# Two edits to a hybrid diffusion step: modulation row SH2 of layer 0 summed by VectorE, and other orders at the changes of phase

## The chip, the cores and the metric

The kernel runs on one core of one Trainium2 chip. Its time is device time in microseconds (us) of one execution of the whole program; the number used is the median of several executions. Five engines work side by side, each on its own queue of instructions: TensorE (PE) does matmuls, VectorE (DVE) and ScalarE (ACT) elementwise work, GpSimd (POOL) and SyncE (SP) issue transfers here. PSUM holds the results of matmuls; the 16 DMA engines move data between main memory and the on-chip SBUF.

## The reference

One step of a two-layer backbone on 128 context tokens and 256 latent tokens (384 columns together), width D = 2048, all in float32:

```python
for l in range(2):
    sh1, sc1, g1, sh2, sc2, g2 = split(silu(cvec) @ w_ada[l] + b_ada[l])   # six rows of 2048 per stream
    h = rmsnorm(x, norm_mix[l]) * (1 + sc1) + sh1
    mix = mixer_ab(h) if l == 0 else pool_mixer(h)   # attention + bidirectional HGRN2, or pooling
    x = x + g1 * mix
    h = rmsnorm(x, norm_mlp[l]) * (1 + sc2) + sh2
    x = x + g2 * (square(relu(h @ w_mlp_in[l])) @ w_mlp_out[l])
return rmsnorm(x, final_norm), new_k, new_v, new_s_fwd, new_s_bwd
```

The HGRN2 mixer keeps a 128x128 state for each of 8 heads in both directions, with forget gates; attention has 8 query heads on 2 key heads. Every row of the six (SH1, SC1, G1, SH2, SC2, G2) is a vector times a matrix of 2048 x 2048, for two vectors: the context's and the latent tokens'.

## The kernel before, in words

**Units and halves.** Weights stream through the chip as a list of items. One unit is 1 MB of weights, loaded by SP into one of three buffers `raw` (L139). A unit has two halves. For an ordinary unit each half is split into two rounded parts, high by ACT (`sp<-raw`, L166) and low by DVE (`sp<-raw`, L173), and PE runs 24 matmuls of 128x384 on them (`acc`, L273, L274, L276), or 36 of 128x256 where tokens are the rows (L403 to L405). Splits run four halves ahead of the matmuls. A `raw` buffer is loaded again only when both halves of its unit have been read, so the unit three places on waits for that.

**Units of the six rows.** An ada unit is 1 MB of `w_ada`. Where PE sums it (`ada_pe`), a unit is one group of four matmuls `psa<-raw,cpad` (L449), four units make a block of 512 columns, and the block is evacuated by ACT (`adarow`) and sent by POOL into the tile `folded`. Where DVE sums it (`ada_dve`), each half is two instructions over 128x1024 (`adaacc`; the first pair of a block TENSOR_SCALAR, L550, the others SCALAR_TENSOR_TENSOR, L552), and after eight units one group of four matmuls adds up the partitions (L566). The work of an ada unit is issued when the splits pass its place in the list, straight behind the low split of the half before it. In layer 0, G1, SH2 and SC2 are summed by PE, as 48 units spread over the mixer's items; G2 and layer 1's rows by DVE during the MLPs.

**Stages.** Start: the tokens are loaded, turned by PE (`px`, L725), their norm computed, SH1 and SC1 summed on PE (L501). Then the mixer of layer 0, 56 items behind the first: pairs of HGRN heads, attention's Q, K and V, four gates, sixteen output units; then MLP 0, pool mixer, MLP 1, final norm.

**An HGRN head** goes through seven levels. At each, PE makes `pl`, DVE updates `arr`, `tot` and `att`, ACT makes `kh`, and PE needs these for the next `pl`. After the last level come the two `arr` instructions (L993, L994), PE's output `po`, ACT's copies `sout`, DVE's `COPY O` (L1011). After two heads a norm follows: ACT's square root `oss` (L1021), DVE's RECIPROCAL and `O<-O,oss` (L1025), then PE's `pbh` (L1029), which stands in PE's queue ahead of the next matmuls.

**A change of phase** (before MLP 0, the pool mixer and MLP 1) computes the norm of `x`: ACT squares it (`sq`), DVE adds the squares (`sqacc`), PE sums over partitions (`pst`, L805), ACT takes the root (`rstd`, L809), DVE its reciprocal, PE spreads it (`pbc`, L827), DVE multiplies (`xnc`), ACT and DVE make `hh` and `hl`. PE runs filler matmuls (`busy`, L822) meanwhile.

Everything is in an order written by hand: a queue per engine, taken from the front. Background tasks (queues e, h, q, f) are advanced at given numbers of ticks.

Of the kernel before, what the change touches and what calls it, by code (L numbers as in the profile page):

```python
# [18 lines left out]
P = 128  # L19
# [20 lines left out]
LEAD = 6  # L40
WARM = (4, 3, 7)
WARM_START = 8
HY1 = 4.0
# [3 lines left out]
SPILL = 10  # L47
RAW_RING = 3
DMA_AHEAD = 6

# [64 lines left out]
class Model:  # L115
    def __init__(self, ctx, tc, a):
        self.ctx, self.tc, self.nc, self.a = ctx, tc, tc.nc, a
        self.items = []
        self.pend = []
        self.sqs = []  # L120
        self.queues = {"e": [], "h": [], "q": [], "f": []}
        self.now = 0.0
# [90 lines left out]
    def run(self):  # L213
# [7 lines left out]
        for j in range(2 * len(self.items)):  # L221
# [28 lines left out]
            if it["kind"] == "a" or (it.get("one") and half):  # L250
# [4 lines left out]
                continue  # L255
            if half == 0 and it["pre"]:
                self.flush()
                it["pre"]()
# [65 lines left out]
    def start_units(self, w, specs, pre=None):  # L324

        tiles = {}

        def make(q, n):
            def proc(half, sp):
                if q == 0:  # L330
                    tiles[n] = self.acc_pair()
                self.quarter_mm(tiles[n], sp, q, q == 0, q == 3)
                if q == 3:
                    self.pend.append(lambda: specs[n][1](tiles[n]))
            return proc

        return [self.quarter(w, specs[n][0], q, make(q, n), pre) for q in range(4) for n in range(len(specs))]

# [97 lines left out]
    def ada_pe(self, layer, which, block, each=None, then=None):  # L436
# [5 lines left out]
        def make(u):  # L442
            def proc(half, raw):
# [11 lines left out]
                if u == 3 and half == 1:  # L455
                    if layer == 0 and which in (SH1, SC1):
                        self.drain("f")
                    rows = self.small.tile([P, 512], F32, name="adarow", tag="adarow")
                    nc.scalar.activation(rows, st["ps"], AF.Copy)
                    if layer == 0 and which in (SH1, SC1):  # L460
                        self.task("f", finish(rows), PSRD)
                        if block == 0:
                            self.drain("f")
                    else:
                        if block == 0:
                            self.folded = self.small.tile([P, P], F32, name="folded", tag="folded", bufs=2)
                        for v in range(2):
                            at = block * 32 + v * 16
                            nc.gpsimd.dma_start(self.folded[at:at + 16], rows[v::32].rearrange("j (n c) -> j n c", n=4))
                        if block == 3:  # L470
                            self.task("f", self.ada_fold(layer, which, 0, P, self.folded), 6.5)
            return proc
# [63 lines left out]
    def ada_dve(self, layer, which, block):  # L536
# [5 lines left out]
        def make(u):  # L542
            def proc(half, raw):
                kc = u * 2 + half
                if kc == 0:
                    st["acc"] = self.mlpp.tile([P, 2, 1024], F32, name="adaacc", tag="adaacc")
                for v in range(2):
                    s = self.cpad[:, kc, v:v + 1]
                    if kc == 0:
                        nc.vector.tensor_scalar(st["acc"][:, v], raw[:, 0], s, None, op0=ALU.mult)  # L550
                    else:
                        nc.vector.scalar_tensor_tensor(st["acc"][:, v], raw[:, 0], s, st["acc"][:, v],  # L552
                                                       op0=ALU.mult, op1=ALU.add)
                if kc == KC - 1:
                    self.task("f", finish(), 4.0)
            return proc

        def finish():
            if block == 0:
                self.folded = self.small.tile([P, P], F32, name="folded", tag="folded", bufs=2)  # L560
            folded = self.folded
            psr = self.ps_a.tile([P, 512], F32, name="psa", tag="a")
            for v in range(2):
# [120 lines left out]
    def start_x(self):  # L684
# [7 lines left out]
        nc.vector.reciprocal(ss, ss)  # L692
        self.ss = ss

    def spread_x(self):
# [4 lines left out]
    def first_work(self, part, i):  # L700

        if part == 0:
            self.turn_x(2 * i)
            self.turn_x(2 * i + 1)
        if (part, i) in self.later:
# [13 lines left out]
    def turn_x(self, kc):  # L719
# [4 lines left out]
        for t in range(3):  # L724
            nc.tensor.transpose(ps[:, t], x[:, t], self.ident)  # L725
        if kc % 2:
            nc.vector.tensor_copy(x, ps)
# [55 lines left out]
    def square_into(self, kcs, late=False):  # L783
# [4 lines left out]
        for kc in kcs:  # L788
            sq = self.sqp.tile([P, T], F32, name="sq", tag="sq", bufs=3)
            nc.scalar.activation(sq, self.x[:, kc], AF.Square)  # L790
            self.sqs.append(sq)
        if kcs[0] < 2 and len(self.sqs) == 2:
            self.sqacc = self.sqp.tile([P, T], F32, name="sqacc", tag="sqacc", bufs=1)
            add(self.sqacc, self.sqs.pop(0), self.sqs.pop(0), op=ALU.add)
        while kcs[0] > 1 and len(self.sqs) > (late or kcs[-1] == KC - 1):
            add(self.sqacc, self.sqacc, self.sqs.pop(0), op=ALU.add)

    def norm(self):

        nc = self.nc  # L800
        self.keep_busy(WARM[0])
        ps = self.ps_s.tile([P, 3, 2], F32, name="pst", tag="s")
        for b in range(3):
            for n, t in enumerate([self.sqacc] + self.sqs):
                nc.tensor.matmul(ps[:, b], t[:, b * P:(b + 1) * P], self.ones[:, 0:2], start=(n == 0),  # L805
                                 stop=(n == 1))
        self.sqs = []
        r = self.tmp.tile([P, 3], F32, name="rstd", tag="rstd", bufs=1)
        nc.scalar.activation(r, ps[:, :, 0], AF.Sqrt, bias=self.eps, scale=1.0 / D)  # L809
        nc.vector.reciprocal(r, r)  # L810
# [407 lines left out]
    def open_mix(self):  # L1218
# [11 lines left out]
        self.nc.gpsimd.dma_start(self.ck, self.a["cache_k"][0, 0])  # L1230
        self.nc.gpsimd.dma_start(self.V[:, 3], self.a["cache_v"][0, 0].rearrange("t h d -> t (h d)"))
        self.hg_ctx = ExitStack()
        self.hg = self.hg_ctx.enter_context(self.tc.tile_pool(name="hgp", bufs=1))
# [6 lines left out]
    def open_x(self):  # L1240
# [6 lines left out]
        self.sqp = xp  # L1247
        self.task("q", self.read_x(), 1.0)

    def read_x(self):  # L1250

        for k in range(0, KC, 4):
            for b in range(3):
                self.nc.gpsimd.dma_start(self.x[:, k:k + 4, b * P:(b + 1) * P],
                                         self.x_spill[:, b, k * P:(k + 4) * P].rearrange("p (k t) -> p k t", t=P))
            yield 3.8

# [18 lines left out]
    def out_jobs(self):  # L1276
        w = self.a["w_out_ab"][0]
        for half, m in ((1, "mixA"), (0, "mixB")):
            for p in range(8):
                def evac(ps, os=(0, 1), p=p, half=half):  # L1280
                    for o in os:
                        self.add_x(2 * p + o, ps[o], self.part(0, G1))
# [90 lines left out]
    def pool_jobs(self):  # L1373
# [4 lines left out]
        for g in range(4):  # L1378
# [27 lines left out]
            src = w[g].rearrange("(k p) c -> p k c", p=P)  # L1406
            self.w_unit(src, (4, 512), proc, self.pool_pre if g == 0 else None)

# [71 lines left out]
    def build(self):  # L1480
# [103 lines left out]
```

## Time and profile before

| | us |
|---|---|
| median of three runs | 3092.82 (3092.79 to 3094.85) |
| the profiled execution, its time | 3093.35 |
| its span in the profile | 3091.6 |
| PE busy | 3041.5 (98%) |
| DVE busy | 1874.4 (61%) |
| ACT busy | 1153.5 (37%) |
| mean granted TensorE clock | 0.997 of full speed |

The profiled execution took 1.75 us more than its span, for what lies around it. The page gives busy time of each engine, the span in 40 slices, the chain of work that ended last, and groups of like instructions; the trace behind it gives every instruction with start, duration and what it waited for.

### The profile page before, as it was taken

Reading aid. Unit: us, or ns where it says so; the run is one execution under the profiler, and the core shown is the slowest. Engines: PE = TensorE matmul, PEld = TensorE weight load, DVE = VectorE, ACT = ScalarE, POOL = GpSimd, SP = SyncE. Lnnn points to the kernel's source line nnn. Section 1 sums busy time; section 2 is a strip of 40 time slices with the busy share of each in tenths; the row PEclk is TensorE's granted clock in tenths of the full one; section 3 lists DMA queues with packets and bytes.
Section 4 is the critical chain, followed back from the end, with each engine's and each line's share of the span. In section 5 each row is a group of like instructions: output and inputs, shape, how many; then the busy total and the mean of one; then the engine's idle time right before and its main releaser. Section 6 shows DMA issues by size and latency. Waiting matters only on the chain.

```text
span 3091.6 us, 43344 instructions
## 1 busy us (share of the span) xinstructions
PE 3041.5 (98%) x18074; PEld 2911.9 (94%) x18074; DVE 1874.4 (61%) x2448; ACT 1153.5 (37%) x1745; POOL 80.3 (3%) x137
## 2 busy tenths in 40 slices
PE   7999999999999999999999999999999999999997
PEld 4898999988999999999999999799999999999997
DVE  3555555555578988898998345754445444443444
ACT  3443333343453333323233333653333323333233
POOL 1100000010000000000000000000000000000000
PEclk9999999999999999999999999999999999999999
DMA  9964555564567777777777454254454444443452
GB/s 339 350 196 163 179 175 176 176 199 160 170 219 247 247 245 245 245 245 245 247 248 248 136 161 129 98 164 140 148 161 152 150 137 158 155 144 123 129 166 80
DMA packets 423764, 579.44 MB, mean 187 GB/s; under 512 B 11432, under 2 KB 348312, under 8 KB 422928
## 3 DMA queue, kind: packets, MB, share of 16 engines
q1 hardware_dynamic: 409728, 543.91, 54.3%
q0 software_dynamic: 8784, 28.29, 2.6%
q10 hardware_dynamic: 5056, 4.47, 0.5%
q8 instruction: 142, 2.33, 0.3%
q14 instruction: 54, 0.44, 0.0%
HBM read 562.42 MB, written 13.89 MB: 186 GB/s over the span
## 4 chain that ended last, share of the span: by engine, by line
PE 95%; DVE 2%; ACT 2%; DMA 1%; issue 0%; SPq 0%; DVEq 0%; ACTq 0%
PE acc L273 28%; PE acc L276 28%; PE acc L274 28%; PE psa L449 2%; PE pl L971 1%; DMA raw<-in_w_ada 1%; PE acc L403 1%; PE acc L405 1%; PE acc L404 1%; PE psa L566 0%; ACT hfull L765 0%; ACT sp L166 0%; PE acc L295 0%; DVE sp L173 0%; PE pov L1209 0%
## 5 line engine op out<-in xcount | busy, mean ns | idle before, releaser
L166 ACT ACTIVATE sp<-raw 128x1024 fp32r<-128x1024 f32 x656 | 694.2, 1059 | 1444.4 <-PE acc L276 1191.0
L173 DVE TENSOR_TENSOR sp<-raw,sp 128x1024 fp32r<-128x1024 f32 x656 | 795.7, 1222 | 590.6 <-ACT sp L166 590.3
L273 PE MATMUL acc<-hh,sp 128*128 128x384 f32 x2720 | 923.3, 339 | 3.2 <-ACT hh L767 1.5
L274 PE MATMUL acc<-hh,sp 128*128 128x384 f32 x2720 | 909.9, 335 | 0.0
L276 PE MATMUL acc<-hl,sp 128*128 128x384 f32 x2720 | 691.3, 335 | 0.0
L273 PE MATMUL acc<-hid,sp 128*128 128x384 f32 x2032 | 686.3, 338 | 0.0
L274 PE MATMUL acc<-hid,sp 128*128 128x384 f32 x2032 | 683.2, 336 | 0.0
L273 PEld LDWEIGHTS acc<-hh,sp 128*128 128x128 f32 x2720 | 510.8, 188 | 51.2 <-issue 39.0
L276 PE MATMUL acc<-hid,sp 128*128 128x384 f32 x2032 | 518.9, 337 | 0.0
L552 DVE SCALAR_TENSOR_TENSOR adaacc<-raw,cpad,adaacc 128x1024 f32<-128x1024 f32 x420 | 511.6, 1279 | 0.0
L274 PEld LDWEIGHTS acc<-hh,sp 128*128 128x128 f32 x2720 | 511.0, 188 | 0.1
L276 PEld LDWEIGHTS acc<-hl,sp 128*128 128x128 f32 x2720 | 491.4, 188 | 0.0
L273 PEld LDWEIGHTS acc<-hid,sp 128*128 128x128 f32 x2032 | 381.4, 188 | 5.9 <-issue 5.9
L274 PEld LDWEIGHTS acc<-hid,sp 128*128 128x128 f32 x2032 | 381.5, 188 | 0.0
L276 PEld LDWEIGHTS acc<-hid,sp 128*128 128x128 f32 x2032 | 367.3, 188 | 0.0
L777 DVE TENSOR_TENSOR hid<-rsq,hid 128x384 fp32r<-128x384 f32 x128 | 65.8, 555 | 195.0 <-ACT hid L776 195.0
L1359 DVE TENSOR_TENSOR x<-acc,x 128x384 f32<-128x384 f32 x192 | 97.8, 551 | 86.9 <-PE acc L276 86.9
L953 ACT ACTIVATE kh<-arr 128x384 f32<-128x384 f32 x56 | 31.2, 558 | 180.0 <-DVE arr L976 80.8
L449 PE MATMUL psa<-raw,cpad 128*32 128x512 f32 x576 | 78.0, 603 | 2.6 <-DMA raw<-in_w_ada 2.6
L976 DVE TENSOR_TENSOR arr<-arr,tot 128x384 f32<-128x384 f32 x96 | 49.2, 554 | 40.9 <-PE pl L971 39.6
L403 PE MATMUL acc<-sp,hh 128*128 128x256 f32 x240 | 72.7, 303 | 0.0
L1337 ACT ACTIVATE rsq<-relu 128x384 f32<-128x384 f32 x128 | 67.4, 526 | 4.1
(283 smaller groups left out, 2139.1 us busy)
## 6 DMA issues: line engine op xcount, KB each, us to landing
raw<-in_w_ada SPq DMA_DIRECT2D x192, 1024.0 KB, 5.1
raw<-in_w_mlp_out SPq DMA_DIRECT2D x128, 1024.0 KB, 5.5
raw<-in_w_mlp_in SPq DMA_DIRECT2D x120, 1024.0 KB, 5.5
raw<-in_w_in_ab SPq DMA_DIRECT2D x42, 1024.0 KB, 5.1
raw<-in_w_out_ab SPq DMA_DIRECT2D x16, 1024.0 KB, 5.6
raw<-in_w_mlp_in SPq DMA_DIRECT2D x16, 512.0 KB, 3.9
raw<-in_w_in_ab POOLq DMA_DIRECT2D x15, 512.0 KB, 7.3
x_kept<-x POOLq DMA_DIRECT2D x8, 768.0 KB, 3.6
```

The lines of the kernel that those rows point to most:

```text
L166: self.nc.scalar.activation(sp[:, 0], raw, AF.Copy)
L173: self.nc.vector.tensor_tensor(sp[:, 1], raw, sp[:, 0].bitcast(F32), op=ALU.subtract)
L273: mm(ps[:, :T], sp[:, 0, kc, c], hi, start=first, stop=False)
L274: mm(ps[:, :T], sp[:, 1, kc, c], hi, start=False, stop=False)
L276: mm(ps[:, :T], sp[:, 0, kc, c], lo, start=False, stop=last)
L403: nc.tensor.matmul(ps, hi, sp[:, 0, kc], start=(gk == 0), stop=False)
L449: nc.tensor.matmul(st["ps"][32 * j:32 * j + 32], self.cpad[:, kc], raw[:, k], start=(u == 0), stop=(u == 3))
L552: nc.vector.scalar_tensor_tensor(st["acc"][:, v], raw[:, 0], s, st["acc"][:, v], op0=ALU.mult, op1=ALU.add)
L777: nc.vector.tensor_tensor(lo, full, hi.bitcast(F32), op=ALU.subtract)
L976: nc.vector.tensor_tensor(x, x, m, op=ALU.mult)
L1337: nc.scalar.activation(q[o], r[o], AF.Square)
L1359: nc.vector.tensor_tensor(self.x[:, kc], ps[o][:, :T], self.x[:, kc], op=ALU.add)
```

## The change

One part hands SH2 of layer 0 to DVE. Its sixteen units go behind items picked by hand (`QUIET`, counted from the first HGRN item of pair 1; a number twice means two units there). G1 and SC2 stay on PE, as 32 units spread over the items. `adaacc` gets its own memory, and the folding matmuls use another PSUM pool.

The other part reorders the changes of phase and the start. In the norm, `pst` runs over the squares in the outer loop and the tokens in the inner one, so that only three matmuls need the last square; before MLP 1 the last four squares aren't added by DVE, and PE sums them (15 matmuls). The norm is issued ahead of the splits of the items that follow ("early"). At the start, four of the sixteen turns of the tokens go ahead of the first SH1 group, with their copies on DVE. The re-read of `x` in the mixer (3 MB) is cut into 24 transfers, three every 6.5 ticks, where 12 went out together. Fillers are fewer (`WARM`, `WARM_START`), and the memory for software DMA descriptors is set to 8192.

```diff
-WARM = (4, 3, 7)
-WARM_START = 8
+WARM = (4, 3, 4)
+WARM_START = 6
+QUIET = (0, 9, 10, 20, 20, 28, 36, 37, 38, 38, 39, 49, 50, 51, 52, 53)
...
-            if half == 0 and it["pre"]:
+            if half == 0 and it["pre"] and "early" not in it:
...
+        units[0]["early"] = pre
...
                 if kc == 0:
-                    st["acc"] = self.mlpp.tile([P, 2, 1024], F32, name="adaacc", tag="adaacc")
+                    self.drain("f")
+                    st["acc"] = self.accp.tile([P, 2, 1024], F32, name="adaacc", tag="adaacc")
...
-            psr = self.ps_a.tile([P, 512], F32, name="psa", tag="a")
+            psr = self.ps_bg.tile([P, 512], F32, name="psa", tag="bg")
...
         self.ss = ss
+        for kc in range(4):
+            self.turn_x(kc)
...
-        if part == 0:
-            self.turn_x(2 * i)
-            self.turn_x(2 * i + 1)
+        if part == 0 and i < 6:
+            self.turn_x(2 * i + 4)
+            self.turn_x(2 * i + 5)
...
-        if kc % 2:
+        if kc % 2 or kc < 4:
             nc.vector.tensor_copy(x, ps)
...
+        if late and kcs[0] >= KC - 4:
+            return
...
-        for b in range(3):
-            for n, t in enumerate([self.sqacc] + self.sqs):
-                nc.tensor.matmul(ps[:, b], t[:, b * P:(b + 1) * P], self.ones[:, 0:2], start=(n == 0),
-                                 stop=(n == 1))
+        for n, t in enumerate([self.sqacc] + self.sqs):
+            for b in range(3):
+                z = 6 + HEADS - 1 - b
+                nc.tensor.matmul(ps, t[:, b * P:(b + 1) * P], self.sel[:, z:z + 4], start=(n == b == 0),
+                                 stop=(n == len(self.sqs) and b == 2))
...
-        for k in range(0, KC, 4):
+        for k in range(0, KC, 2):
             for b in range(3):
...
-            yield 3.8
+            self.x_read += 1
+            yield 6.5
...
-        self.items = mix[:n0] + spread(mix[n0:], pe(G1, SH2, SC2), 0, len(mix) - n0 - 3)
+        body, quiet = mix[n0:], dve((0, SH2))
+        steps = len(body) - 3
+        own = pe(G1, SC2)
+        out, done = [], 0
+        for n, it in enumerate(body):
+            want = min(n * len(own) // steps, len(own))
+            out += own[done:want]
+            done = want
+            out.append(it)
+            for _ in range(QUIET.count(n)):
+                out.append(quiet.pop(0))
+        self.items = mix[:n0] + out + own[done:] + quiet
...
-    nc = _bacc.Bacc("TRN2", target_bir_lowering=False, num_devices=1)
+    nc = _bacc.Bacc("TRN2", target_bir_lowering=False, num_devices=1, dynamic_dma_scratch_size=8192)
```

The first place where the order moves is DVE at the end of the fourth HGRN head and the norm of that pair (`O<-po` is the head's output, `oss` the norm's factor, `pbh` comes from PE). Before:

```order
297 L993 TENSOR_SCALAR arr<-arr,tot 128x128
298 L994 TENSOR_SCALAR arr<-arr,tot 128x128
299 L173 TENSOR_TENSOR sp<-raw,sp 128x1024
300 L1011 COPY O<-po 128x384
301 L1022 RECIPROCAL oss<-oss 128x6
302 L1025 TENSOR_TENSOR O<-O,oss 128x384
```

After:

```order
298 L1004 TENSOR_SCALAR arr<-arr,tot 128x128
299 L1005 TENSOR_SCALAR arr<-arr,tot 128x128
300 L558 SCALAR_TENSOR_TENSOR adaacc<-raw,cpad,adaacc 128x1024 x8
301 L175 TENSOR_TENSOR sp<-raw,sp 128x1024
302 L1022 COPY O<-po 128x384
303 L1033 RECIPROCAL oss<-oss 128x6
304 L1036 TENSOR_TENSOR O<-O,oss 128x384
```

Two units of SH2, eight instructions, now stand between the head's last `arr` and its `COPY O`.

The second place is DVE at the end of the last head, with the same names. Before:

```order
480 L994 TENSOR_SCALAR arr<-arr,tot 128x128
481 L1011 COPY O<-po 128x384
482 L173 TENSOR_TENSOR sp<-raw,sp 128x1024
483 L1022 RECIPROCAL oss<-oss 128x6
484 L1025 TENSOR_TENSOR O<-O,oss 128x384
```

After:

```order
485 L1005 TENSOR_SCALAR arr<-arr,tot 128x128
486 L1022 COPY O<-po 128x384
487 L556 TENSOR_SCALAR adaacc<-raw,cpad 128x1024 x2
488 L558 SCALAR_TENSOR_TENSOR adaacc<-raw,cpad,adaacc 128x1024 x6
489 L175 TENSOR_TENSOR sp<-raw,sp 128x1024
490 L1033 RECIPROCAL oss<-oss 128x6
491 L1036 TENSOR_TENSOR O<-O,oss 128x384
```

Here the two units stand behind `COPY O` and ahead of the norm that PE's next `pbh` needs.

The third place is the start of PE's queue (`px` turns tokens, `psa` is a group of SH1). Before:

```order
1 L634 MATMUL pvec<-mats,vrows 128x32
2 L501 MATMUL psa<-raw,cpad 32x256 x4
3 L725 MATMUL px<-mats,xtok 128x128 x6
4 L501 MATMUL psa<-raw,cpad 32x256 x4
5 L725 MATMUL px<-mats,xtok 128x128 x6
```

After:

```order
1 L640 MATMUL pvec<-mats,vrows 128x32
2 L733 MATMUL px<-mats,xtok 128x128 x12
3 L506 MATMUL psa<-raw,cpad 32x256 x4
4 L733 MATMUL px<-mats,xtok 128x128 x6
5 L506 MATMUL psa<-raw,cpad 32x256 x4
```

Twelve turns, four chunks of the tokens, now stand ahead of the first group.

## Rows read from the trace of the kernel before

**Rows 1.** The page: busy time, share of span, instructions of each engine.

```profile
PE 3041.5 (98%) x18074; PEld 2911.9 (94%) x18074; DVE 1874.4 (61%) x2448; ACT 1153.5 (37%) x1745; POOL 80.3 (3%) x137
```

**Rows 2.** Windows: from:to, length, busy of each engine, clock, DMA share, GB/s.

```profile
0.00:50.00 50.00, 32.07 (x252) 21.85 (x256) 17.76 (x43) 25.34 (x40) 8.22 (x20) 1.00 0.97 344
1925.00:2003.00 78.00, 70.48 (x371) 58.99 (x369) 54.64 (x116) 49.98 (x91) 2.15 (x4) 0.98 0.30 102
```

**Rows 3.** Timeline, PE, 256 to 270: start, duration, instruction, [idle before <- releaser].

```profile
258.21 0.83 PE L971 MATMUL pl<-arr,kh 128*128 128x128 f32 x6
...
263.07 0.83 PE L971 MATMUL pl<-arr,kh 128*128 128x128 f32 x6
263.83 1.06 PE L449 MATMUL psa<-raw,cpad 128*32 128x512 f32 x8
...
269.12 0.83 PE L971 MATMUL pl<-arr,kh 128*128 128x128 f32 x6
```

**Rows 4.** Groups, shapes apart: count, busy and mean ns of one, idle before.

```profile
L552 DVE SCALAR_TENSOR_TENSOR adaacc<-raw,cpad,adaacc 128x1024 f32<-128x1024 f32 x420 | 511.6, 1279 | 0.0
...
L550 DVE TENSOR_SCALAR adaacc<-raw,cpad 128x1024 f32<-128x1024 f32 x28 | 19.7, 747 | 0.0
```

**Rows 5.** Timeline, DVE and PE, 402 to 423: end of the fourth head.

```profile
407.20 0.28 DVE L994 TENSOR_SCALAR arr<-arr,tot 128x128 f32<-128x128 f32 x1
...
413.94 0.56 DVE L1011 COPY O<-po 128x384 f32<-128x384 f32 x1 [2.80 <-ACT sout L1010]
...
416.52 0.56 DVE L1025 TENSOR_TENSOR O<-O,oss 128x384 f32<-128x384 f32 x1
...
417.67 0.49 PE L1029 MATMUL pbh<-mats,O 128*128 128x128 f32 x3
```

**Rows 6.** Timeline, DVE and PE, 500 to 513: end of the sixth head.

```profile
503.96 0.59 DVE L958 COPY_PREDICATED att<-masks,pl 128x384 f32<-128x384 uint8 x1
...
509.54 0.39 PE L1001 MATMUL po<-s,arr 128*128 128x128 f32 x2
```

**Rows 7.** Timeline, DVE, ACT and PE, 612 to 646: end of the last head.

```profile
624.56 0.56 DVE L1011 COPY O<-po 128x384 f32<-128x384 f32 x1 [4.28 <-ACT sout L1010]
...
628.95 0.56 DVE L1025 TENSOR_TENSOR O<-O,oss 128x384 f32<-128x384 f32 x1
...
627.10 1.28 ACT L1021 ACT_TABLE_LOAD   x1
...
630.05 0.49 PE L1029 MATMUL pbh<-mats,O 128*128 128x128 f32 x3
```

**Rows 8.** DMA issues: count, size of one, median us from issue to landing.

```profile
raw<-in_w_ada SPq DMA_DIRECT2D x192, 1024.0 KB, 5.1
```

**Rows 9.** Timeline, PE, 650 to 674: all its waits.

```profile
656.44 1.07 PE L449 MATMUL psa<-raw,cpad 128*32 128x512 f32 x8 [2.26 <-DMA raw<-in_w_ada]
672.02 0.46 PE L1207 MATMUL pov<-probt,V 128*128 128x128 f32 x2 [0.56 <-DVE probt L1200]
```

**Rows 10.** Timeline, PE and DVE, 12 to 40: the start.

```profile
15.65 1.08 PE L501 MATMUL psa<-raw,cpad 128*32 128x256 f32 x8 [11.41 <-DMA raw<-in_w_ada]
...
18.73 0.17 DVE L692 RECIPROCAL ss<-ss 128x3 f32<-128x3 f32 x1 [13.63 <-ACT ss L691]
...
19.15 1.54 PE L725 MATMUL px<-mats,xtok 128*128 128x128 f32 x6
...
36.62 0.42 PE L273 MATMUL acc<-hh,sp 128*128 128x384 f32 x1
```

**Rows 11.** Waits of SP's queue, 0 to 60: total us, times, longest.

```profile
SPq L139 <- PE psa L501: 18.6, 7, 3.6
```

**Rows 12.** Changes of phase, timeline and chain: start, duration, what.

```profile
834.75 1.06 ACT L166 ACTIVATE sp<-raw 128x1024 fp32r<-128x1024 f32 x1 [0.57 <-PE acc L295]
...
836.24 1.28 ACT L809 ACT_TABLE_LOAD   x1
...
1994.16 1.50 PE pst L805 x12
```

More of the change, by code (lines that the diff above doesn't have):

```diff
@@ L120, in __init__ @@
         self.sqs = []
-        self.queues = {"e": [], "h": [], "q": [], "f": []}
+        self.folded = {}
+        self.queues = {"e": [], "h": [], "q": [], "f": [], "x": []}
         self.now = 0.0
@@ L335, in make @@
             return proc
-        return [self.quarter(w, specs[n][0], q, make(q, n), pre) for q in range(4) for n in range(len(specs))]
+        units = [self.quarter(w, specs[n][0], q, make(q, n), pre) for q in range(4) for n in range(len(specs))]
+        units[0]["early"] = pre
+        return units
     def first_units(self, w, specs):
@@ L465, in proc @@
                         if block == 0:
-                            self.folded = self.small.tile([P, P], F32, name="folded", tag="folded", bufs=2)
+                            self.folded[layer, which] = self.small.tile([P, P], F32, name="folded", tag="folded", bufs=3)
+                        folded = self.folded[layer, which]
                         for v in range(2):
                             at = block * 32 + v * 16
-                            nc.gpsimd.dma_start(self.folded[at:at + 16], rows[v::32].rearrange("j (n c) -> j n c", n=4))
+                            nc.gpsimd.dma_start(folded[at:at + 16], rows[v::32].rearrange("j (n c) -> j n c", n=4))
                         if block == 3:
-                            self.task("f", self.ada_fold(layer, which, 0, P, self.folded), 6.5)
+                            self.task("f", self.ada_fold(layer, which, 0, P, folded), 6.5)
             return proc
@@ L559, in finish @@
             if block == 0:
-                self.folded = self.small.tile([P, P], F32, name="folded", tag="folded", bufs=2)
-            folded = self.folded
-            psr = self.ps_a.tile([P, 512], F32, name="psa", tag="a")
+                self.folded[layer, which] = self.small.tile([P, P], F32, name="folded", tag="folded", bufs=3)
+            folded = self.folded[layer, which]
+            psr = self.ps_bg.tile([P, 512], F32, name="psa", tag="bg")
             for v in range(2):
@@ L788, in square_into @@
         for kc in kcs:
-            sq = self.sqp.tile([P, T], F32, name="sq", tag="sq", bufs=3)
+            sq = self.sqp.tile([P, T], F32, name="sq", tag="sq", bufs=5)
             nc.scalar.activation(sq, self.x[:, kc], AF.Square)
@@ L801, in norm @@
         self.keep_busy(WARM[0])
-        ps = self.ps_s.tile([P, 3, 2], F32, name="pst", tag="s")
-        for b in range(3):
-            for n, t in enumerate([self.sqacc] + self.sqs):
-                nc.tensor.matmul(ps[:, b], t[:, b * P:(b + 1) * P], self.ones[:, 0:2], start=(n == 0),
-                                 stop=(n == 1))
+        ps = self.ps_s.tile([P, 4], F32, name="pst", tag="s")
+        for n, t in enumerate([self.sqacc] + self.sqs):
[3 more added lines that the diff above has]
+                                 stop=(n == len(self.sqs) and b == 2))
         self.sqs = []
         r = self.tmp.tile([P, 3], F32, name="rstd", tag="rstd", bufs=1)
-        nc.scalar.activation(r, ps[:, :, 0], AF.Sqrt, bias=self.eps, scale=1.0 / D)
+        nc.scalar.activation(r, ps[:, :3], AF.Sqrt, bias=self.eps, scale=1.0 / D)
         nc.vector.reciprocal(r, r)
@@ L1231, in open_mix @@
         self.nc.gpsimd.dma_start(self.V[:, 3], self.a["cache_v"][0, 0].rearrange("t h d -> t (h d)"))
+        self.accp = self.ctx.enter_context(self.tc.tile_pool(name="accp", bufs=1))
         self.hg_ctx = ExitStack()
@@ L1247, in open_x @@
         self.sqp = xp
-        self.task("q", self.read_x(), 1.0)
+        self.x_read = 0
+        self.task("x", self.read_x(), 1.0)
     def read_x(self):
-        for k in range(0, KC, 4):
+        for k in range(0, KC, 2):
             for b in range(3):
-                self.nc.gpsimd.dma_start(self.x[:, k:k + 4, b * P:(b + 1) * P],
-                                         self.x_spill[:, b, k * P:(k + 4) * P].rearrange("p (k t) -> p k t", t=P))
-            yield 3.8
+                self.nc.gpsimd.dma_start(self.x[:, k:k + 2, b * P:(b + 1) * P],
+                                         self.x_spill[:, b, k * P:(k + 2) * P].rearrange("p (k t) -> p k t", t=P))
+            self.x_read += 1
+            yield 6.5
     def after_in(self):
@@ L1280, in evac @@
                 def evac(ps, os=(0, 1), p=p, half=half):
+                    while self.x_read <= p:
+                        self.advance(self.queues["x"])
                     for o in os:
@@ L1406, in pool_jobs @@
             src = w[g].rearrange("(k p) c -> p k c", p=P)
-            self.w_unit(src, (4, 512), proc, self.pool_pre if g == 0 else None)
+            self.w_unit(src, (4, 512), proc)
+            if g == 0:
+                self.items[-1]["early"] = self.pool_pre
     def make_more(self, n):
```

## Prediction

> **What bounds the kernel now.** I read the busy shares first: PE works 98% of the span, DVE 61%, ACT 37% [rows 1]. 3091.6 less 3041.5 leaves 50 us in which PE is idle. The windows say where: 50.0 less 32.1, so 17.9 us, in the first 50 us, and 78.0 less 70.5, so 7.5 us, at the pool mixer between 1925 and 2003 [rows 2]. The mixer of layer 0, where SH2 is summed, has nearly no idle time. So there are two ways to gain: take matmuls off PE, or shorten the waits at the start and the changes of phase. The danger is that an engine with 39% of free time isn't free where PE waits for it. I therefore looked next at the order of DVE's queue and, with the timeline, at what PE asks of DVE behind each block of new work.
>
> **SH2 off PE.** Sixteen groups of four matmuls go, two groups that fold DVE's sums come, of the same four-matmul form: fourteen less. What a group costs PE I read from a pair of HGRN levels. Level to level takes 263.07 less 258.21, 4.86 us, with 24 ordinary matmuls and no group, and 269.12 less 263.07, 6.05 us, with the same 24 and one group [rows 3]. The difference is 1.19 us, and 14 x 1.19 = 16.7 us. The group's own record in that stretch lasts 1.06 us [rows 3], so the sum by records would be 14.8 us. The Trainium skill (Perfetto Trace Analysis, Tensor Engine Instruction (MATMUL, LD_WEIGHTS)) says that TensorE's recorded end is computed from the size of the instruction and not observed, which speaks for the distance between starts; by it the term is -16.7, by the records -14.8. I take -16.7.
>
> **What DVE gets for it.** 64 instructions: 4 x 0.747 + 60 x 1.279 = 79.7 us [rows 4]. A unit of four is 5.1 us, 4.05 where it opens a block. DVE's queue is in order, so what stands behind a block waits for it. Per place:
>
> Behind item 20 stand two units, 8 x 1.279 = 10.2 us, directly behind the head's last `arr`, which ends at 407.5 [rows 5]. They end at 407.5 + 10.2 = 417.7. Behind them come a low split (1.14), `COPY O` (0.47), the reciprocal (0.2) and `O<-O,oss` (0.56): 420.1. PE's `pbh` needed it at 417.67, and earlier by the group that no longer stands ahead of it, 416.5 [rows 5]. PE stalls 3.6 us.
>
> Behind item 38 stand a unit that opens a block and one that doesn't, 4.05 + 5.1 = 9.2 us, between `COPY O` (ends 625.1) and the norm [rows 7]. 625.1 + 9.2 = 634.3, low split 1.14, reciprocal 0.2, `O<-O,oss` 0.56: 636.2, where PE's `pbh` stood at 630.05 [rows 7]. That is 6.1 us. It may be more. The next ordinary unit's load takes the buffer of the first of the two, free at 625.1 + 4.05 = 629.2, and lands 5.1 us later [rows 8], 634.3; ACT's split (1.06 [rows 12]) stands in its queue ahead of the table load (1.28 [rows 7]) and the root (0.3), then DVE's 0.2 + 0.56: 637.7, 7.6 us. I take the middle, 6.9.
>
> Behind item 28 stands one unit behind `att` (ends 504.55): 504.55 + 5.1 = 509.7, a low split 1.14, two `arr` of 0.3: 511.4, where PE's `po` wanted `arr` at 509.54 [rows 6]. 1.9 us.
>
> Behind items 36 and 37 a unit each lies in a level; by the same comparison each pushes PE 0.3 us, bounded by 0 and the 1.9 of item 28: 0.6 together. Behind items 9 and 10 the blocks themselves fit, but the load three units on waits for a buffer until the block is through; between 0 and the 5.1 us of a load [rows 8], I take 1.3, near the low end, as splits run four halves ahead. Behind item 0, behind item 39, where DVE rests, and behind 49 to 53 I find no stall: in the output units the block and DVE's own work fill about one item's time, and the additions to x may come late while a second pair of `acc` is free. Cover gone, these six could cost up to 1.9 us each, as at item 28.
>
> Together 3.6 + 6.9 + 1.9 + 0.6 + 1.3 = 14.3 us, bounded by 5 (if half of item 38's stall and nearly all of the others is covered) and 20.
>
> **The start.** Twelve transposes now stand ahead of the first SH1 group, which ran at 15.65 when its weights landed [rows 10]. Their copies are on DVE, behind the reciprocal of `ss` at 18.73 [rows 10]. Two PSUM buffers take the first two chunks; the third waits for a copy, 18.9 + 0.56 = 19.5, and the pair 1.5 us at that pace (1.54 [rows 10]). So the first group runs at about 20.8, 5 us later. The transposes had stood between groups and aren't lost, but SP waits for these groups: 18.6 us in seven waits for buffers that `psa` holds [rows 11], while DMA is busy 97% of the stretch [rows 2]. The transfers under way cover part of the 5 us. Two pairs of transposes fewer later give 1.6, fewer fillers 0.5. The first `acc` at 36.62 [rows 10] comes between 0.5 earlier (all of it covered) and 5 later; I take 3 later, as the waits for buffers say that DMA can't run ahead.
>
> **Changes of phase.** Before MLP 1 `pst` took 1.50 us, twelve records, behind the last sum of squares [rows 12]; now six stand behind the last square: 0.75 less. Skipping the four additions gives little, as PE's own pooling matmuls pace the additions to x. Before the pool mixer the same order gives 0.5 by the same records, and the split that stood ahead of the square 0.2, but that split of 1.06 now lies inside a stretch where ACT and DVE set the pace: 0.3 left. Before MLP 0 the table load, 836.24 to 837.52, ends as late as `pst` does [rows 12], so the shorter `pst` is hidden and only the 0.2 of the moved split stays. Sum 1.25, taken as 1.5; bounds 0 and 3.5, under half the 7.5 us of idle time at the pool mixer [rows 2].
>
> **The re-read of x.** A transfer of `w_ada` landed late behind the burst, and PE waited 2.26 us at 656.44; it then waited again at 672.02 for DVE's `probt` [rows 9], on a chain through ACT and DVE that began before. Removing the first wait lengthens the second. I take 0.3, bounds 0 and 2.3. The smaller descriptor memory, the earlier folds and the moved PSUM tile I put at nothing: the transfers that use them have ticks to spare; without that cover each fold's wait would be of the size of one landing, 5 us [rows 8], three times at most.
>
> **The sum.** -16.7 + 14.3 + 3 - 1.5 - 0.3 = -1.2 against the profiled 3093.35, so 3092.2. The median of the runs shown lies 0.5 lower: 3091.6, which I give as 3091.5.
>
> **Rivals.** (1) *Cover.* The blocks cost 5 and not 14.3, since stalls at one place give DVE time at the next: 9.3 less, 3082.2. For it: DVE is free 39% of the time. Against it: items 20 and 38 are chains of known durations on one queue. (2) *Short chains work.* The start is 0.5 earlier and the phases give 3.5: 5.5 less, 3086. For it: 17.9 and 7.5 us of idle time lie there. Against it: the first group stands behind DVE's copies. (3) *Buffers of raw weights, slower.* A unit on DVE holds its buffer until its four instructions have run, where PE freed it in 1.2 us; the unit three places on lands 5.1 us after that [rows 8], and ACT's queue stands at its split while HGRN waits for `kh`. If it bites at items 9, 10, 20, 36 and 37 with 2.5 us each, 12.5 less the 1.9 counted: 10.6 more, 3102. It decides where DVE ends the block later than 5.1 + 1.06 us before that split is due. Against it: the splits' lead.
>
> **Chances.** Forecast 0.48 (its own range 3087 to 3097), cover 0.20, short chains 0.14, buffers 0.18. About 0.2%, 6.2 us, is what a measurement here can tell from no change: faster is under 3086.6, slower over 3099.0. Faster: all of the cover, half of the short chains, a little of the forecast, 0.31. Slower: nearly all of the buffers and the forecast's upper end, 0.20. The range goes from the cover's 3082 to the buffers' 3102.
>
> **What would show it.** `psa` groups of L449 fewer by 64 matmuls. PE idle ahead of `pbh` at the fourth and the last head, of 3 to 4 and 6 to 8 us, and 2 us at the sixth head's `po`, released by DVE. The first SH1 group at 20 to 21 us and the first `acc` at 39 to 40. `pst` behind the last square 0.75 us. I am wrong if PE doesn't wait at those two `pbh`, or if the first `acc` comes at 36.

## The result, and the profile after

The changed kernel takes 3113.08 us (median of five runs, 3107.31 to 3120.46) against 3094.38 before in the same comparison: 1.0061 of the time, 95% interval 1.0049 to 1.0072. It is slower by 19 us. The prediction was 3091.5 with a range up to 3102, so it was wrong: it forecast a small gain, and even its upper end lies 11 us below. The profiled run spans 3111.3 us.

The page of the changed kernel, the line that answers to [rows 1]:

```profile
PE 3034.9 (98%) x17964; PEld 2916.6 (94%) x17964; DVE 1944.4 (62%) x2510; ACT 1150.9 (37%) x1741; POOL 84.0 (3%) x143
```

PE's busy time fell by only 6.6 us and the span grew by 19.7, so 26 us of idle time came in. DVE got 70.0 us more busy; its `adaacc` instructions kept their lengths, 1278 and 746 ns against the 1279 and 747 of [rows 4]. To place the loss I cut both traces at four events that every version has: PE's first `acc`, its first `pst` on the last square ahead of MLP 0 and ahead of the pool mixer, and the `pbc` ahead of MLP 1. Before, they come at 36.62, 836.28, 1930.16 and 1996.27; after, at 39.18, 844.04, 1944.68 and 2015.79. What is left to the end of the span, 1095.3 and 1095.5, is alike.

| us | first `acc` | mixer | MLP 0 | pool mixer and norm |
|---|---|---|---|---|
| before | 36.6 | 799.7 | 1093.9 | 66.1 |
| after | 39.2 | 804.9 | 1100.6 | 71.1 |
| difference | +2.6 | +5.2 | +6.8 | +5.0 |
| predicted | +3 | -2.9 | 0 | -1.3 |

Each stage has a loss of its own. (In the prediction's row the 0.2 us at MLP 0's norm lie with the mixer.) The window from 50 to 826 us, before and then of the changed kernel (columns as in [rows 2]), gives PE's idle time in the mixer, 7.5 us and then 24.5:

```profile
50.00:826.00 776.00, 768.51 (x4937) 681.13 (x4936) 422.96 (x773) 283.73 (x475) 41.99 (x66) 1.00 0.61 202
50.00:826.00 776.00, 751.49 (x4800) 676.38 (x4793) 491.08 (x835) 279.67 (x469) 46.75 (x72) 1.00 0.60 201
```

The list of PE's waits in that window, of the changed kernel (waiting instruction, releaser, us in total, times, longest):

```profile
PE psa L453 <- DMA raw<-in_w_ada: 4.8, 4, 2.7
PE pbh L1040 <- ACT sp L168: 4.4, 1, 4.4
PE pqs L1108 <- ACT qsq L1105: 3.4, 1, 3.4
PE pbh L1040 <- DVE O L1036: 3.3, 2, 2.8
PE po L1013 <- DVE arr L1005: 2.5, 1, 2.5
PE pov L1218 <- DVE probt L1211: 1.4, 1, 1.4
```

The stalls that the prediction named are there, each at its place: `pbh` of the fourth head 2.8, `po` of the sixth 2.5, `pbh` of the last 4.4. The timeline of DVE, ACT and PE around the last head shows how, against [rows 7]:

```profile
624.39 0.56 DVE L1022 COPY O<-po 128x384 f32<-128x384 f32 x1 [3.40 <-ACT sout L1021]
624.87 1.41 DVE L556 TENSOR_SCALAR adaacc<-raw,cpad 128x1024 f32<-128x1024 f32 x2
626.19 7.26 DVE L558 SCALAR_TENSOR_TENSOR adaacc<-raw,cpad,adaacc 128x1024 f32<-128x1024 f32 x6
633.36 1.22 DVE L175 TENSOR_TENSOR sp<-raw,sp 128x1024 fp32r<-128x1024 f32 x1
634.81 0.19 DVE L1033 RECIPROCAL oss<-oss 128x6 f32<-128x6 f32 x1 [0.23 <-ACT oss L1032]
635.04 0.56 DVE L1036 TENSOR_TENSOR O<-O,oss 128x384 f32<-128x384 f32 x1
...
635.74 0.87 PE L1040 MATMUL pbh<-mats,O 128*128 128x128 f32 x3 [4.44 <-ACT sp L168]
```

From 624.9 to 633.4 DVE runs the two units, then the split, the reciprocal and the product, and PE's `pbh` follows 0.14 us behind. The reciprocal still waited 0.23 us for ACT's root, which was late because ACT's split had waited for a load until 632.1: ACT's chain and DVE's block arrive together. The releaser that the list names is ACT's `sp`, which ended at 635.73; `pbh` reads `O`, which DVE finished at 635.60, 0.13 us earlier.

### The profile page after: what moved, and what is told of

It reads as the page before. It is cut to its first block, busy times and chain, and to the rows that moved or that the text cites. A ratio compares the mean times of both kernels' runs of the same rounds, so it can differ in the third digit from the quotient of the medians.

```text
span 3111.3 us, 43189 instructions
## 1 busy us (share of the span) xinstructions
PE 3034.9 (98%) x17964; PEld 2916.6 (94%) x17964; DVE 1944.4 (62%) x2510; ACT 1150.9 (37%) x1741; POOL 84.0 (3%) x143
## 4 chain that ended last, share of the span: by engine, by line
PE 55%; issue 23%; DVE 2%; DMA 2%; ACT 1%; POOL 0%; DVEq 0%; POOLq 0%; ACTq 0%
PE acc L275 17%; PE acc L276 17%; PE acc L278 17%; DMA raw<-in_w_ada 1%; DVE sp L175 1%; DMA raw<-in_w_in_ab 1%; ACT sp L168 0%; DVE adaacc L558 0%; PE psa L453 0%; ACT hfull L773 0%; PE pov L1220 0%; DVE x L862 0%; PE acc L407 0%; PE acc L297 0%; PE acc L409 0%
## 5 line engine op out<-in xcount | busy, mean ns | idle before, releaser
L558 DVE SCALAR_TENSOR_TENSOR adaacc<-raw,cpad,adaacc 128x1024 f32<-128x1024 f32 x480 | 584.4, 1278 | 0.6 <-DMA raw<-in_w_ada 0.6
L407 PE MATMUL acc<-sp,hh 128*128 128x256 f32 x240 | 73.4, 306 | 0.8 <-DVE hq L895 0.8
L408 PE MATMUL acc<-sp,hh 128*128 128x256 f32 x240 | 68.5, 285 | 0.0
```

The source lines that it names most:

```text
L407: nc.tensor.matmul(ps, hi, sp[:, 0, kc], start=(gk == 0), stop=False)
L408: nc.tensor.matmul(ps, hi, sp[:, 1, kc], start=False, stop=False)
```

## The experiments

Where nothing else is said, the runs stand beside runs of the kernel before on the same chip. The table of stages, worked out from each trace as above, comes first, since most of what follows is read in it. Each of its rows is one traced execution, and the last column the median of all.

| us | first `acc` | mixer | MLP 0 | pool mixer and norm | time (median) |
|---|---|---|---|---|---|
| c1 SH2 on PE, rest changed | 39.4 | 799.5 | 1098.0 | 69.8 | 3104.18 |
| c2 SH2 on DVE, rest as before | 35.9 | 804.8 | 1100.4 | 66.0 | 3104.65 |
| c3 fold's first step only | 39.4 | 804.0 | 1094.0 | 70.0 | 3106.33 |
| c4 last squares added by DVE | 39.2 | 807.9 | 1094.7 | 67.0 | 3105.26 |
| c5 one unit at a place | 35.7 | 804.0 | 1094.1 | 65.9 | 3098.23 |
| c6 start as before | 35.7 | 805.4 | 1099.8 | 69.9 | 3108.62 |
| c7 fillers in two waits | 38.9 | 799.8 | 1102.6 | 68.9 | 3108.2 (one execution) |
| c8 c4, pool's norm not early | 39.2 | 804.4 | 1100.0 | 66.0 | 3105.96 |
| c9 other places | 38.1 | 794.2 | 1094.1 | 66.0 | 3088.91 |
| c10 other places again | 38.2 | 792.0 | 1094.1 | 65.5 | 3085.42 |
| c11 no SH2 on DVE, the rest mended | 39.6 | 799.3 | 1094.1 | 65.8 | 3094.21 |
| c12 c10 with the changed start | 38.1 | 792.0 | 1094.1 | 66.0 | 3088.87 |
| c13 c10 again | 35.6 | 792.4 | 1094.1 | 65.5 | 3086.11 |

**The two parts apart.** c1 puts SH2 back on PE:

```diff
...
-        self.items = mix[:n0] + out + own[done:] + quiet
+        self.items = mix[:n0] + spread(mix[n0:], pe(G1, SH2, SC2), 0, len(mix) - n0 - 3)
```

> The changed kernel with SH2 of layer 0 back on PE as before; start, folds, norms and re-read of x as changed. Theory (each place has its own loss, as the two traces differ: start +2.6 us, mixer +5.2, MLP 0's folds +6.8, pool mixer and the norm behind it +5.0): the mixer's part goes, so about 14 us slower than before, near 3108. Rival (the loss comes with SH2 on DVE, whose stalls disturb all that follows): within 3 us of before.

Measured: 3104.18 against 3092.51, 1.0034 (1.0021 to 1.0047), 11.7 us slower. The part called shorter chains is by itself a loss. Some 4 us of it are the forced fold, which c1 keeps (MLP 0 1098.0 against 1093.9); the start and the pool mixer make most of the rest. c2 is the other part alone, with the start, the norms, the re-read of x and the fillers as before (the smaller descriptor memory stays), and of the change this:

```diff
...
+        self.items = mix[:n0] + out + own[done:] + quiet
```

> The kernel before with SH2 of layer 0 summed by DVE at the same places and the forced fold, but start, norms and re-read of x as before. Theory: mixer +5.2 and MLP 0's folds +6.8 stay, start and pool's losses go: 12 us slower than before, near 3106. Rival (SH2 on DVE is the cause of all): about 19 slower, near 3113.

Measured: 3104.65 against 3092.51, 1.0038 (1.0023 to 1.0053), 12.1 us. Mixer and MLP 0 show the changed kernel's times, start and pool mixer those of before. So each stage's loss goes with the edits made in it; the two medians' losses sum to 24, more than 19, as both kernels have the forced fold.

**The forced fold.** c3 lets a new block force only the four matmuls and the transfer, after whose issue `fold_open` is false:

```diff
...
-                    self.drain("f")
+                    while self.fold_open:
+                        self.advance(self.queues["f"])
...
+                    self.fold_open = True
...
+            self.fold_open = False
...
```

> The changed kernel, in which a new block of sums on DVE forces only the first step of the fold before it (the four matmuls and the transfer), not the matmul that waits for the transfer. Theory: PE's four waits for the folded tile in MLP 0 and the clock's dip behind one of them go, 6.8 us: near 3106. Rival (the small descriptor memory makes the transfer late): the waits appear later or stay, near 3113.

Measured: 3106.33, 6.8 us below the changed kernel's median, whose own runs spread by 13 us; the stage is what tells: MLP 0 takes 1094.0, and 1093.9 before. The list of PE's waits in MLP 0, 850 to 1920, of the changed kernel:

```profile
PE psr L537 <- DMA folded<-adarow: 4.9, 4, 1.9
PE acc L275 <- ACT hh L775: 0.4, 1, 0.4
```

In c3 that list is empty. The waits and a fall of the clock behind one of them (0.83 from 1030 to 1040, 1.7 us) account for the 6.8. `drain("f")` issued not only the fold that had to come first but also the next one, `psr`, which needs a transfer of POOL that has just gone out. c3 keeps the small descriptor memory, so that isn't the cause.

**The last squares.** c4 undoes one line of the norm:

```diff
-        if late and kcs[0] >= KC - 4:
-            return
```

> The changed kernel, in which DVE adds the last four squares before MLP 1 again, so that three matmuls and not fifteen stand behind. Theory (the 24 more records of pst lie on the path, since PE comes to them when the last square is ready): 3.5 to 4 us faster than the changed kernel, near 3109. Rival (the squares, not PE, set the end): no change, 3113.

Measured: 3105.26; from the pool mixer's `pbc` to MLP 1's 65.6 us against 69.7, 4.1 less (before: 64.2). PE's timeline of the changed kernel, then of c4, ahead of MLP 1, against the last of [rows 12]:

```profile
2008.90 0.73 PE L816 MATMUL pst<-mats,sqacc 128*128 128x4 f32 x6
2009.49 5.02 PE L816 MATMUL pst<-mats,sq 128*128 128x4 f32 x30
```

```profile
2006.75 0.83 PE L814 MATMUL pst<-mats,sqacc 128*128 128x4 f32 x6 [0.36 <-DVE sqacc L804]
2007.44 0.81 PE L814 MATMUL pst<-mats,sq 128*128 128x4 f32 x6
```

In the changed kernel ACT's last square is done at 2009.3 and PE first comes to `pst` at 2008.9, behind its pooling matmuls and fillers. So the thirty records for the squares lie on the path nearly whole, 5.0 us, where they and the sum's had been 1.5. Part of the 5.0 is the clock. c7 has the same norm, and PE's timeline has there

```profile
2006.07 3.49 PE L816 MATMUL pst<-mats,sq 128*128 128x4 f32 x30
```

The two windows over these records, of the changed kernel and of c7, show why:

```profile
2009.50:2014.50 5.00, 5.00 (x33) 5.00 (x32) 0.00 (x0) 0.00 (x0) 0.00 (x1) 0.67 0.38 157
2006.00:2009.50 3.50, 3.50 (x33) 3.50 (x33) 0.00 (x0) 0.00 (x0) 0.08 (x1) 1.00 0.58 226
```

From `pbc` to `pbc` c7 takes 67.4 us. So of the 4.1 us that c4 saves, 1.8 are the records at the full clock and 2.3 came with the clock's fall, ahead of which PE had not waited (4.92 us busy in the 5 us from 2005). c4's trace also has fewer fold waits, 0.7 us in MLP 0; what its other runs had was not seen.

**The early norm of the pool mixer.** c8 is c4 with the norm in its old place there:

```diff
-            if g == 0:
-                self.items[-1]["early"] = self.pool_pre
+            self.w_unit(src, (4, 512), proc, self.pool_pre if g == 0 else None)
```

> The kernel with the last squares added by DVE again, and the pool mixer's norm no longer early. Theory (the split that was moved behind the norm lies on the chain of ACT and DVE in the pool mixer): from the pool mixer's pbc to MLP 1's pbc 64.2 us as before, against 65.6 with the early norm, 69.7 in the changed kernel. Rival (the moved split costs nothing): 65.6 again.

Measured: `pbc` to `pbc` 64.5 us, 1.1 less than c4; the six later traces with the old place (c5, c9 to c13) have 64.1 to 64.6. Two rows of PE's waits between 1920 and 2030, of c4 and then of c8:

```profile
PE acc L1409 <- DVE hl L777: 5.0, 6, 1.6
```

```profile
PE acc L1409 <- DVE hl L777: 3.7, 5, 1.6
```

The split that was moved had lain in an ACT rest, and came to lie ahead of `hfull` and `hl`, for which PE waits. The medians, 3105.96 and 3105.26, differ by less than their spread and tell nothing; only the stage does.

**The clock after a wait.** c7 puts fillers where PE waits anyway, ahead of the last head's `pbh` and of the first `pqs` of a new K:

```diff
+            if pair == 3 and h == 6:
+                self.keep_busy(16)
             pb = self.ps_bg.tile([P, T], F32, name="pbh", tag="bg")
...
+                if new_k and o == 0:
+                    self.keep_busy(12)
...
```

> The changed kernel with 16 filler matmuls ahead of the last pair's first pbh and 12 ahead of K's pqs, where PE waits 4.4 and 3.4 us anyway. Theory (the granted clock falls after PE has rested some us, and halves PE's pace for about 5 us): clock 1.00 in 280 to 290 and 630 to 640, where the changed kernel has 0.83, and some 3 us less by the first norm. Rival (the clock falls for another reason): the clock is 0.83 there again.

Measured: windows of the changed kernel, then of c7:

```profile
280.00:290.00 10.00, 9.90 (x61) 8.33 (x62) 6.13 (x8) 3.37 (x5) 0.00 (x0) 0.83 0.33 107
630.00:640.00 10.00, 5.56 (x27) 5.24 (x25) 7.55 (x9) 3.58 (x4) 0.00 (x0) 0.83 0.73 258
```

```profile
280.00:290.00 10.00, 9.71 (x72) 8.30 (x73) 7.60 (x11) 4.16 (x6) 0.00 (x0) 1.00 0.34 107
630.00:640.00 10.00, 9.20 (x63) 7.88 (x62) 8.97 (x12) 3.41 (x5) 0.18 (x1) 1.00 0.73 241
```

A mean of 0.83 over 10 us is a third of the stretch at the lower level, 1.2 GHz. With the fillers, which cost nothing as PE waits anyway, it is 1.00, and the mixer takes 799.8 and not 804.9. The dip at half the pace for a third of 10 us costs 1.7 us in each place, 3.4 together. Of the other 1.7 us, 1.5 lie at the sixth head's `po`, which waits 1.0 us in c7 and 2.5 in the changed kernel; no filler stands there, and the cause of that part is not shown. The clock also differs between traces with one order of the mixer: added up over windows of 10 us, what is missing to 1.00 is 3.4 us in c3 (mixer 804.0) and 10.2 in c4 (807.9), some of it while PE waits.

**Other places.** c5 has one unit at a place and none at three of the stalls, besides the mends of c3, c4, c6 and c8:

```diff
...
-QUIET = (0, 9, 10, 20, 20, 28, 36, 37, 38, 38, 39, 49, 50, 51, 52, 53)
+QUIET = (0, 1, 10, 20, 30, 36, 37, 39, 47, 48, 49, 50, 51, 52, 53, 54)
...
```

> SH2 on DVE with one unit at a place and none behind items 9, 28 and 38 (behind 0, 1, 10, 20, 30, 36, 37, 39 and 47 to 54), the start as before, only the fold's first step forced, the last squares added by DVE, the pool mixer's norm not early. Theory (the loss in the mixer is the stalls behind a few blocks and the clock's dips after them, the rest were the start, the folds, pst and the early norm): saving 15 less some 4 us of small stalls, near 3083. Rival (a block costs a few us wherever it stands): near 3095.

Measured: 3098.23 against 3094.16, 1.0014 (1.0005 to 1.0024): far from the theory's 3083, and above the rival's 3095. All stages but the mixer are as before, and the mixer is no better, 804.0: behind items 1, 47 and 48 three new stalls came. In its trace PE waits 3.9 us at 188.71 for ACT's `hi` and 2.7 and 2.4 at 739.25 and 755.92 for DVE's `probt`, each with a dip of the clock. At the first, ACT's split had waited 7.3 us for a load that went out at 182.22, when the block of item 1 gave its buffer back. So the stalls were not bound to the places left out. c9 and c10 moved these units, from c5 to c9 and from c9 to c10:

```diff
-QUIET = (0, 1, 10, 20, 30, 36, 37, 39, 47, 48, 49, 50, 51, 52, 53, 54)
+QUIET = (0, 10, 14, 20, 24, 30, 33, 35, 37, 39, 49, 50, 51, 52, 53, 54)
```

```diff
-QUIET = (0, 10, 14, 20, 24, 30, 33, 35, 37, 39, 49, 50, 51, 52, 53, 54)
+QUIET = (0, 10, 16, 20, 24, 30, 35, 37, 39, 49, 50, 51, 52, 53, 54, 55)
```

> As the kernel with SH2's units one at a place, but none behind items 1, 47 and 48; instead behind 14, 24, 33 and 35, inside HGRN levels (36 left out): 0, 10, 14, 20, 24, 30, 33, 35, 37, 39 and 49 to 54. Theory (a block costs what stands behind it on DVE, and inside a level that is little): from first acc to MLP 0's pst 792 us (804 with the places before this, 799.7 with SH2 on PE), so near 3086. Rival (every block inside HGRN costs some 2 us and the clock's dip): 799 or more, 3093 to 3096.

> The same with units behind 16 and 55 in place of 14 and 33. Theory: as that one, near 3086; a unit behind the last item but none is free as those behind 49 to 54. Rival: 3093 to 3096.

Measured: c9 3088.91 against 3093.40, 0.9983 (0.9975 to 0.9992); c10 3085.42, 0.9974 (0.9964 to 0.9984). c10's list of waits in the mixer begins so:

```profile
PE psa L575 <- DVE adaacc L560: 1.9, 1, 1.9
PE psa L454 <- DMA raw<-in_w_ada: 1.8, 2, 1.0
PE t L1206 <- issue: 1.3, 1, 1.3
```

No wait is over 2 us, every 10 us from 40 to 830 has a clock of 1.00, and the window as above reads

```profile
50.00:826.00 776.00, 762.61 (x4869) 686.22 (x4868) 498.31 (x846) 286.26 (x477) 46.19 (x73) 1.00 0.60 201
```

so 13.4 us of idle time. c9 kept one wait of 3.5 us, `pck` for DVE's `K`, which stands right behind the block of item 33 (555.19 to 560.06), with one dip; c10 has no unit there, and 792.0 against 794.2. c10 beats both kernels.

c11 has SH2 on PE and of the other edits only those that no trace speaks against, in c10's form (the norm, the early norm ahead of the MLPs, the re-read of x, the fold); its edit of c10:

```diff
...
+        self.items = mix[:n0] + spread(mix[n0:], pe(G1, SH2, SC2), 0, len(mix) - n0 - 3)
```

> SH2 on PE as before, and of the other edits only those that the traces clear: the norm's pst with tokens in the inner loop, the early norm before both MLPs, the re-read of x in 24 pieces, the fold with only its first step forced; start, last squares and the pool's norm as before. Theory: 0.2 us at MLP 0 and 0.75 each at the pool mixer and MLP 1 remain, 1 to 2 us faster than before, 3092. Rival (the table load and the waits behind hide it): no change.

Measured: 3094.21 against 3093.40, 0.9999 (0.9990 to 1.0008): no change. What is left of the shorter chains gains nothing that shows.

**The start.** c6 has only the start as before:

```diff
...
-        for kc in range(4):
-            self.turn_x(kc)
...
-        if part == 0 and i < 6:
-            self.turn_x(2 * i + 4)
-            self.turn_x(2 * i + 5)
+        if part == 0:
+            self.turn_x(2 * i)
+            self.turn_x(2 * i + 1)
...
```

> The changed kernel with the start as before. Theory (the first SH1 group waits for transposes that wait for DVE's copies, and SP's loads for the group): first acc at 36 instead of 39 us, 2.5 to 3 us faster than the changed kernel. Rival (the DMA engines set the start, the order doesn't matter): no change.

Measured: 3108.62 (3103.76 to 3113.23), first `acc` at 35.7. The runs of both spread by some 10 us and overlap, so the median alone proves nothing. With the start as before the first `acc` also came at 38.1, 38.2 and 39.6 (c9 to c11), but in these three the clock fell ahead of it. The windows from 25 to 35 us of c13, c10 and c11, all with the start as before:

```profile
25.00:35.00 10.00, 8.04 (x75) 5.30 (x75) 5.31 (x12) 4.68 (x10) 0.00 (x0) 1.00 1.09 384
25.00:35.00 10.00, 8.31 (x66) 4.82 (x65) 4.17 (x8) 3.57 (x7) 0.00 (x0) 0.83 1.08 381
25.00:35.00 10.00, 8.31 (x53) 4.84 (x52) 3.61 (x7) 3.23 (x7) 0.00 (x0) 0.68 1.09 384
```

The five traces with the old start and a clock of 1.00 there have the first `acc` at 35.6 to 36.6; the seven with the changed start, all at 1.00, at 38.1 to 39.4. c12 and c13 settle it in one comparison, on the kernel without stalls, whose runs spread by 5 us: c13 is c10 itself, and c12 is c10 with the changed start (its fewer fillers too), so with

```diff
...
+        for kc in range(4):
+            self.turn_x(kc)
...
```

> The fastest placing of SH2 so far (behind 0, 10, 16, 20, 24, 30, 35, 37, 39 and 49 to 55) with the changed start. Theory (the first SH1 group at 21 us and not 15.7 delays SP's loads): first acc at 39, and 1 to 3.5 us slower than the same kernel with the start as before. Rival (the start as before also came out at 38 to 39.6 in some traces, so the order doesn't set it): the same time within 1 us.

> The same placing with the start as before, on the same chip in the same rounds. Theory: near 3085 again, first acc between 35.7 and 38.2. Rival: as the kernel with the changed start, within 1 us.

Measured: c12 3088.87 (0.9986, 0.9977 to 0.9995), c13 3086.11 (0.9978, 0.9969 to 0.9987), first `acc` 38.1 and 35.6. The changed start costs 2.8 us by the medians, in line with the 2.4 of the first `acc`. PE's timeline of the changed kernel, against [rows 10]:

```profile
19.54 1.54 PE L733 MATMUL px<-mats,xtok 128*128 128x128 f32 x6 [4.97 <-DVE xtok L735]
21.01 1.08 PE L506 MATMUL psa<-raw,cpad 128*32 128x256 f32 x8
```

The third chunk waits 4.97 us for DVE's copies, the first group runs at 21.0 (predicted 20.8), and SP waits longer for buffers, against [rows 11]:

```profile
SPq L141 <- PE psa L506: 25.3, 7, 7.3
```

## Why the prediction was wrong, point by point

Three steps failed: the forced fold, put at nothing, cost 6.8 us; the changes of phase, put at a gain of 1.5, cost 5.0 from the pool mixer on; and in the mixer, put at a gain of 2.9, the saving was taken too high, the stalls too low, and the clock was left out, so that it lost 5.2. Of the signs that the prediction named, all came but one, the `pst` ahead of MLP 1, and the waits at the two `pbh` were shorter than named. They lay where the sum had a price, and the fold had none. Of the rivals, short chains is refuted by c1 and c11, and the 5 us of cover fit c10's places (13.4 - 7.5 = 5.9 us of idle time) and not the picked ones.

**SH2 off PE, -16.7: too much.** In the mixer's window PE's idle time rose from 7.5 to 24.5 us, 17.0 more, and the clock took 3.4; the stage grew by 5.2. So the saving was 17.0 + 3.4 - 5.2 = 15.2 us. c10, with 13.4 us of idle time and no dip, gives 13.4 - 7.5 + 7.7 = 13.6. The price can be read from the group itself: in [rows 3] it starts at 263.83, and the next line of that timeline is

```profile
264.83 0.44 PE L273 MATMUL acc<-hh,sp 128*128 128x384 f32 x1
```

So a group holds PE for 1.00 us, as do the other undivided groups of the trace, and fourteen for 14.0. The other 0.19 us by which the two levels differ isn't the group's. The Trainium skill (Perfetto Trace Analysis, Tensor Engine Instruction (MATMUL, LD_WEIGHTS)) says that a recorded end of TensorE is computed. The trace agrees: the record, 1.06, is 0.06 longer than the distance of starts across the group. So that distance was the right thing to take, but not across a pair of levels.

**Stalls, +14.3: right in kind, low in size.** Item 20: 3.6 predicted, 2.8 measured; the sum of durations, 10.2, was too long for the block, as instructions that follow one another overlap:

```profile
406.87 9.65 DVE L558 SCALAR_TENSOR_TENSOR adaacc<-raw,cpad,adaacc 128x1024 f32<-128x1024 f32 x8
```

Item 28: 1.9, 2.5. Item 38: 6.9, and 4.4 + 1.2, as PE waited 1.2 us for a late load of its own just before; the block took 8.6 us and not 9.2. Item 9: ACT's split at 277.82 waited 2.4 us for its load, and K's `pqs` behind it cost 3.4 (before 0.9), where I had 1.3 with item 10. Items 49 to 53, which I put at nothing because DVE's work fits there, made two of PE's groups wait for loads, 0.6 and 2.7 us: I counted DVE's time and left out that a unit on DVE holds its buffer for 5 us. Their loads went out at 780.25 and 789.76, when two of DVE's blocks ended, and landed at 785.31 and 797.65. There, and at item 1 in c5, the rival on buffers was right in mechanism. At 9 and 38 a load came late too, but not by the block: these loads went out at 272.77, behind the low split of an ordinary unit, and at 627.00, behind PE's own late group. With the small rest, the idle time is 17.0.

**The clock: left out.** After two of these waits PE went on at the lower clock level for a while, 3.4 us in the mixer, and 1.7 after a fold wait at 1030. c7 shows it. The prediction priced a wait at its own length; a wait of 3 to 5 us cost up to 1.7 more.

**The fold: put at nothing, +6.8.** I wrote that without cover each fold's wait would be the size of a landing, three times at most, and took zero because the transfers have ticks to spare. They had them before; the forced `drain` takes them away. The order of PE's queue showed `psr` 18 matmuls behind the fold instead of 42 at five places, at 0.17 us each 3.1 us against a median landing of 4.7: enough to price it. This step failed by not being followed through.

**Changes of phase, -1.5: wrong in sign, +5.0.** At MLP 1 I saw that PE's pooling matmuls pace the additions to x, so that skipping DVE's additions gains nothing, and then counted only six records behind the last square. But the same fact says that PE is not free to run the other 24 before it: 4.1 us by c4, of which 2.3 with the clock. At the pool mixer I priced the moved split's 1.06 us on the chain of ACT and DVE, and it cost 1.1 (c8), where I had left a gain of 0.3. The 0.2 at MLP 0 is lost in the noise.

**The start, +3: right.** 2.4 to 2.8 us by c12 and c13, by the mechanism named. **The re-read of x, -0.3:** the wait of 2.3 at 656 went, a new one of 1.3 came at 673.58 (`t`), and that of `pov` grew from 0.6 to 1.4 (677.99), much as the prediction said; c11 shows no gain.

The sum: the mixer came out 8 us worse, the folds 6.8, the pool mixer with its norms 6.3, together the 21 us between -1.2 and +19.7. The spread of the changed kernel's runs, 13 us against 2 before, fits with fold waits and clock dips that differ from trace to trace (0.7 to 5.6 us of fold waits in MLP 0; 3.4 to 10.2 us missing to the full clock in the mixer), but which runs had which was not seen.

## What to carry to other kernels

An engine's free time is worth nothing by its share: what counts is what stands behind the new work on that queue, how long it keeps a buffer of the ring, and whether the engine that waits falls to a lower clock. Work moved to a rest should go in pieces no longer than the rest, and each piece needs a look at the chain behind it; moving the same sixteen units to other places turned +5 us into -8. When a barrier is added for one dependency, list everything that it flushes.

## What the runs showed of the hardware

The granted clock fell from 2.4 to 1.2 GHz for part of the 10 us behind PE waits of 3.4 and 4.4 us in the changed kernel, but behind the wait of 2.8 us at 418.95 it stayed at 1.00 there, and fell to 0.83 at 420 to 430 in c4's trace, with the same order. Waits of under 2 us in c10's mixer left it at 1.00, but behind a fold wait of 1.9 us in the changed kernel it was 0.83 (1030 to 1040), and over the thirty `pst` records ahead of MLP 1 it was 0.67 though PE had not waited. So in these traces the length of the one wait before does not settle it. Fillers in the wait kept it up in c7. The stretch from the start to the first `acc` came out between 35.6 and 39.6 us with one and the same order at the start, and the late ones are those in which the clock fell to 0.83 or 0.68 between 25 and 35 us. What made it fall there was not found: PE's longest wait between 20 and 30 us is 0.85 us in c10, and 0.85 in c13, where it did not fall. All three late traces come from one chip, and every other trace whose chip is on record comes from another.
